# One trunk layer of an mLSTM, Conformer and DiT hybrid: seven products for eight in two more f tiles, the convolution norm's rows spread by transfers, and four smaller edits

## The chip, the cores and the metric

The kernel runs on one core of one Trainium2 chip. The metric is the device time of one execution in microseconds; lower is better. The engines are named as the profile names them: PE is TensorE (matrix products), DVE is VectorE, ACT is ScalarE, POOL is GpSimd, and SP is SyncE, which here only issues transfers.

## What is computed

One layer runs over 128 context tokens and 512 latent tokens with the same weights, in float32. `D_MODEL` is 1024, `D_FF` 2816, the mLSTM has 4 heads of 128, the Conformer branch 512 channels and a convolution of 31 taps.

```python
h = rmsnorm(x, p['norm1_g']) * (1 + sc1) + sh1
proj = jnp.einsum('btd,dc->btc', h, p['w_in']) + p['b_in']
q, k, v, o, i_f, f_f, i_b, f_b, u, ga, gb = jnp.split(proj, offs, axis=-1)
hA, st_f, st_b = mlstm_bidir(heads(q) * (DH_A ** -0.5), heads(k), heads(v),
                             gts(i_f), gts(f_f), gts(i_b), gts(f_b), st_f, st_b)
...
branch_a = jnp.einsum('bte,ed->btd', jax.nn.sigmoid(o) * hA, p['w_proj_a'])
ua, ub = jnp.split(u, 2, axis=-1)
z = dwconv1d(ua * jax.nn.sigmoid(ub), p['conv_dw_w'], p['conv_dw_b'])
z = jax.nn.silu(layernorm(z, p['conv_ln_g'], p['conv_ln_b']))
branch_b = jnp.einsum('bte,ed->btd', z, p['w_proj_b'])
merged = jax.nn.sigmoid(ga) * branch_a + jax.nn.sigmoid(gb) * branch_b
x = x + g1 * jnp.einsum('btd,de->bte', merged, p['w_out'])
h2 = rmsnorm(x, p['norm2_g']) * (1 + sc2) + sh2
gate, val = jnp.split(jnp.einsum('btd,df->btf', h2, p['w_up']), 2, axis=-1)
gate = dwconv(gate)          # 3x3 on the latent grid, width 3 on the context
x = x + g2 * jnp.einsum('btf,fd->btd', jax.nn.gelu(gate) * val, p['w_down'])
y = rmsnorm(x, final_norm_g)
```

The six modulation vectors (`sc1`, `sh1`, `g1` and their like) come from a linear map of SiLU(c). Outputs are y and the mLSTM's final context state.

## The kernel before

**Layout.** x stands feature-major: eight tiles of 128 features by 640 tokens. All weights are one array of blocks of 128 x 128, in the order in which they are used; eight blocks are a group (`GB`, 512 KB). SP loads groups into a ring of three tiles, `wst` (`load`, L459).

**Products.** Every large product is made from two roundings of each operand, a high part and the low rest. `prep` (L474) makes them of a weight group: ACT copies `wst` to `wh`; the low part `wl` is either `wst - wh` on DVE, or, for the groups in the set `TWICE` (L163), ACT writes the negative of the copy to `wl` and POOL issues a transfer that adds the group from device memory (`in_w`) to it. `three_of` (L623) then issues three matmuls for each block and each half of 320 tokens: high by high, high weight by low input, low weight by high input. The `h` of the input projection is split alike into `hh` and `hl`, those of the FFN stand in one tile `h`, or `hx` below.

**Order.** Each engine works its instructions in program order. The order is made while the program is built: `_Order` (L187) keeps a clock of its own for each engine, with a cost for each operation (`cost`, L220). Between the matmuls it resumes generators (`od.spawn`), which yield until what they wait for is ready by that clock (`until`, L305) or until DVE is not too far ahead (`room`, L313), and it fills DVE with small pieces of background work (`later` and `fill`, L339 and L342): the taps of both convolutions and the products of the later modulation, `junk` in the profile.

**Stages.** Input projection in the order of `ORDER` (u, g, k, q, ...; k and q with number 2 are the third heads'), the mLSTM beside it, then both branches (`BRANCH`), w_out, the FFN, and the final norm.

**The convolution norm** (`conv_norm`, L1260) is a layer norm over 512 channels, which lie in the partitions of four tiles z. PE sums over partitions (`colsum_into`, L665: a row of 656 columns as 4 groups of 164, at partitions 0, 32, 64 and 96), DVE makes the mean `mu`, and `bcast` (L670) spreads that row over all partitions by four matmuls into two PSUM tiles, from which DVE subtracts, in halves of 328 columns. The squares are summed in the same way, and `bcast` spreads the reciprocal deviation.

**The FFN.** D_FF is 22 f tiles of 128. A tile's up projection gives gate and value, 128 x 640 each. For f below `NPL` (L57) `ffn_tile` (L1628) makes it with eight products per pair of k blocks and two token halves, 96 matmuls in all. For the others `ffn_pair` (L1638) makes it with seven, in the way of Strassen: gate and value rows, and the two halves of tokens, form a 2 x 2 scheme over each pair of k blocks. The seven weight forms are A11, S1, S2, A12, S3, S4, A22 (`FORMS`); S1 to S4 are sums and differences of weights, `sf` in the profile, made and split by `prep_form` (L505): for S1 and S3 the low part is made on DVE, for the others by an adding transfer of POOL's. They meet the input forms B11, T1, T2, B21, T3, B22, T4. B's are quarters of h2. T1 to T4 are differences of them, 4 forms for 4 k pairs, that is 16 tiles `hx`. The generator `up_forms` (L1501) makes them: DVE the difference (`hf`), ACT its high part, DVE the low part (`hx<-hf,hx`). They come in the order T1, T3, T2, T4 for the first k pair, then for the next. `ffn_pair` waits for all of them in the order's clock (`od.finish(t_uf)`) before it issues its products. Each product of a weight form runs over its four k pairs, 4 x 3 = 12 matmuls. The gate is collected in `gbuf`, the nine taps of its convolution are DVE's (`acc`). Parts of the down product stand between f tiles (`DN_AT`): the first one behind f4.

**The end.** The down product's last part runs over the tokens in two parts, 384 and 256. `final` (L1749) norms each part: sums over partitions by `colsum_into`, `rstd` (L681) with a reciprocal and four small operations on DVE, a spread by matmuls, and the products that give y.

**PSUM** is set up by `psum_pools` (L392): a pool `mm` for products and a pool `ps` for all else.

## Time and profile before

| what | us |
|---|---|
| runs | 949.36, 950.96, 951.27 |
| median | 950.96 |
| the profiled execution | 950.29 |
| its span | 948.5 |
| PE busy in it | 914.2 |
| DVE busy | 742.1 |
| ACT busy | 531.6 |
| POOL busy | 130.6 |

The span runs from the first to the last recorded instruction; times in the profile count from its start. All instructions go through one helper, so the profile gives the line L182 for nearly all of them, and they are told apart by tile names: `mm<-hx,wl` is a product into PSUM tile mm of the inputs hx and wl. A row of the timeline gives start, duration, engine, line, operation and tiles; a run of like instructions is one row with its count. In square brackets stands how long the engine sat idle before it and what ended that.

### The profile page before, as it was taken

To read this page: it belongs to the slowest core of one execution; us is meant where nothing else is said; L and a number is where in the kernel's file an instruction comes from. 1 tells how busy PE (TensorE), PEld (TensorE's weight loads), DVE (VectorE), ACT (ScalarE), POOL (GpSimd) and SP (SyncE) were. 2 spreads that over 40 slices of the span, in tenths; PEclk is the share of its full clock that TensorE was granted. 3 is DMA by queue.
4 is the path that set the end of the run, shared out by engine and by line. 5 is a ranking of instruction groups with operands and counts; after the bars stand their busy time and mean duration, and the time that the engine had idled before them with its cause. 6 is when DMAs were issued, how large, how long until landed. Compare 5 with 4: busy or idle time off the path is not lost.

```text
span 948.5 us, 16981 instructions
## 1 busy us (share of the span) xinstructions
PE 914.2 (96%) x6456; PEld 893.0 (94%) x6456; DVE 742.1 (78%) x1540; ACT 531.6 (56%) x995; POOL 130.6 (14%) x181
## 2 busy tenths in 40 slices
PE   5999997999999999999999999999999999999995
PEld 2899997999999999999999999999999999999995
DVE  3829777887857988889788996877778877878666
ACT  5564575267758222223478766646765666666662
POOL 0001212000000000000000112222222222222210
PEclk9999999899999999999999999999999999999998
DMA  9638939543215646667544769887888889889975
GB/s 356 264 121 170 241 96 264 129 101 89 79 46 166 202 154 196 205 204 257 172 156 133 166 143 201 169 179 169 183 171 183 174 172 183 176 175 185 206 166 150
DMA packets 65954, 164.90 MB, mean 174 GB/s; under 512 B 6864, under 2 KB 15824, under 8 KB 65872
## 3 DMA queue, kind: packets, MB, share of 16 engines
q1 hardware_dynamic: 41360, 113.20, 37.0%
q0 software_dynamic: 24512, 50.60, 31.5%
q8 instruction: 51, 0.84, 0.4%
q14 instruction: 31, 0.25, 0.1%
HBM read 151.39 MB, written 3.48 MB: 163 GB/s over the span
## 4 chain that ended last, share of the span: by engine, by line
PE 83%; DMA 6%; DVE 4%; ACT 3%; issue 2%; SPq 0%; DVEq 0%; POOLq 0%; POOL 0%; ACTq 0%
PE mm L182 64%; PE ps L182 19%; DMA wl<-in_w 2%; DMA E<-in_mask 1%; DMA rowM<-M 1%; DMA out_ocst<-cs 1%; DMA x<-in_xT 1%; ACT L182 1%; DMA E<-rowM 1%; DVE x L182 0%; ACT z L182 0%; SPq L182 0%; DVE wl L182 0%; DMA cb<-in_crow 0%; DVE bc L182 0%
## 5 line engine op out<-in xcount | busy, mean ns | idle before, releaser
L182 ACT ACTIVATE wh<-wst 128x1024 fp32r<-128x1024 f32 (+1 forms) x114 | 114.1, 1007 | 99.2 <-PE mm L182 85.9
L182 DVE SCALAR_TENSOR_TENSOR acc<-gbuf,cols,acc 128x455 f32<-128x455 f32 (+2 forms) x176 | 129.7, 740 | 14.8 <-ACT acc L182 12.4
L182 PE MATMUL mm<-hh,wl 128*128 128x320 f32 (+2 forms) x576 | 134.8, 313 | 5.6 <-DMA wl<-in_w 5.6
L182 PE MATMUL mm<-hh,wh 128*128 128x320 f32 (+2 forms) x576 | 134.3, 312 | 2.9 <-ACT hh L182 1.6
L182 PE MATMUL mm<-hl,wh 128*128 128x320 f32 (+2 forms) x576 | 134.9, 313 | 0.0
L182 DVE SCALAR_TENSOR_TENSOR z<-glu,cols,z 128x641 f32<-128x641 f32 (+14 forms) x120 | 102.4, 887 | 22.6 <-ACT z L182 21.6
L182 POOL DMA_DIRECT2D wl<-in_w x69 | 60.9, 883 | 390.3 <-ACT wl L182 225.5
L182 PEld LDWEIGHTS mm<-hh,wl 128*128 128x128 f32 x576 | 97.0, 190 | 7.1 <-DMA wl<-in_w 5.9
L182 PEld LDWEIGHTS mm<-hh,wh 128*128 128x128 f32 x576 | 97.7, 190 | 4.8 <-ACT hh L182 2.1
L182 PEld LDWEIGHTS mm<-hl,wh 128*128 128x128 f32 x576 | 97.1, 190 | 1.8 <-issue 1.3
L182 PE MATMUL mm<-h,wh 128*128 128x320 f32 x452 | 85.5, 310 | 1.4 <-ACT h L182 0.8
L182 DVE SCALAR_TENSOR_TENSOR junk<-ad,cb 128x512 bf16<-128x512 f32 x128 | 82.0, 685 | 0.0
L182 DVE TENSOR_TENSOR wl<-wst,wh 128x1024 fp32r<-128x1024 f32 x55 | 67.1, 1221 | 17.2 <-ACT wh L182 17.1
L182 PE MATMUL mm<-al,wh 128*128 128x320 f32 (+2 forms) x336 | 80.5, 309 | 0.0
L182 PE MATMUL mm<-ah,wh 128*128 128x320 f32 (+2 forms) x336 | 80.3, 309 | 0.0
L182 PE MATMUL mm<-ah,wl 128*128 128x320 f32 (+2 forms) x336 | 80.3, 308 | 0.0
L182 ACT ACTIVATE wl<-wst 128x1024 fp32r<-128x1024 f32 (+1 forms) x91 | 74.3, 840 | 4.7 <-PE mm L182 4.7
L182 PEld LDWEIGHTS mm<-h,wh 128*128 128x128 f32 x452 | 71.2, 188 | 2.7 <-DVE h L182 1.2
L182 PE MATMUL mm<-h,wl 128*128 128x320 f32 x364 | 73.1, 309 | 0.3 <-DMA wl<-in_w 0.3
L182 DVE SCALAR_TENSOR_TENSOR x<-mm,mods,x 128x128 f32<-128x128 f32 (+1 forms) x168 | 63.7, 433 | 8.1 <-PE mm L182 7.5
L182 PEld LDWEIGHTS mm<-h,wl 128*128 128x128 f32 x364 | 58.5, 188 | 0.6 <-DMA wl<-in_w 0.6
L182 PEld LDWEIGHTS mm<-ah,wh 128*128 128x128 f32 x336 | 57.2, 188 | 0.1
(249 smaller groups left out, 1930.6 us busy)
## 6 DMA issues: line engine op xcount, KB each, us to landing
wst<-in_w SPq DMA_DIRECT2D x138, 512.0 KB, 4.5
wl<-in_w POOLq DMA_DIRECT2D x47, 512.0 KB, 7.2
ad<-in_ada SPq DMA_DIRECT2D x64, 256.0 KB, 3.1
adst<-in_ada SPq DMA_DIRECT2D x16, 512.0 KB, 10.2
wf<-in_w POOLq DMA_DIRECT2D x23, 256.0 KB, 5.0
wh<-sf POOLq DMA_DIRECT2D x22, 256.0 KB, 5.3
wl<-in_w POOLq DMA_DIRECT2D x22, 256.0 KB, 6.0
x<-in_xT SPq DMA_DIRECT2D x16, 320.0 KB, 5.8
```

What stands on the lines that cost most here:

```text
L182: return fn(*args, **kw)
```

## The change

1. `NPL` goes from 5 to 3: the f tiles 3 and 4 (the fourth and fifth) are made by `ffn_pair`. The wait for the sixteen T forms therefore comes at f3 and not at f5.
2. The weight groups of k and q with number 2 leave `TWICE`: DVE makes their low part from the tile in SBUF, where ACT's second copy and POOL's transfer made it.
3. Where each PSUM tile is one bank, the pool `ps` is opened before `mm`, so their banks change places.
4. Of the squares of x, tiles 3, 4, 5 and 7 are made by DVE; the first group's split stands behind the first `mrows`.
5. `on_all` takes the place of `bcast` in the convolution norm: SP writes the row to device memory (`zrow`) and reads it back into all partitions (`zb`). DVE subtracts and multiplies 656 columns at once, from SBUF.
6. The end's second part sums with tokens in the partitions (`token_sums`, two columns in place of 64), and `token_rows` spreads the result by two matmuls with the identity.

```diff
-NPL = 5
+NPL = 3
...
+TWICE -= {_g for _g in _IN if BLOCKS[_g * GB][0] in ("k", "q") and BLOCKS[_g * GB][2] == 2}
...
-        pools["mm"] = st.enter_context(tc.tile_pool(name=f"mm{nmm}", bufs=nmm, space=bass.MemoryType.PSUM))
-        pools["ps"] = st.enter_context(tc.tile_pool(name=f"ps{nps}", bufs=nps, space=bass.MemoryType.PSUM))
+        for nm, n in (("mm", nmm), ("ps", nps))[::-1 if banks == 1 else 1]:
+            pools[nm] = st.enter_context(tc.tile_pool(name=f"{nm}{n}", bufs=n, space=bass.MemoryType.PSUM))
...
+    def token_sums(pc, tile_, w, first, last):
+
+        n = w // P
+        for c in range(n):
+            PE.matmul(pc[:, c:c + 1], lhsT=tile_[:, c * P:(c + 1) * P], rhs=ones32[:, 0:1], start=first and c == 0,
+                      stop=last and c == n - 1)
+
+    def token_rows(r, a, b):
+
+        pt = ps()
+        for c in range(a, b):
+            PE.matmul(pt[:, (c - a) * P:(c - a + 1) * P], lhsT=r[:, c:c + 1].to_broadcast([P, P]), rhs=ident,
+                      start=True, stop=True)
+        return pt[:, 0:(b - a) * P]
...
-        S.activation(sq, x[j], AF.Square)
-        if j == 3:
+        if j in (3, 4, 5, 7):
+            V.tensor_mul(sq, x[j], x[j])
+        else:
+            S.activation(sq, x[j], AF.Square)
+        if j == 2:
...
-    prep(0)
...
+    prep(0, wait=False)
+    od.force(lines[0])
...
+    def on_all(r):
+
+        d = dz.tile([4, nz], F32, tag="row", name="zrow")
+        Q.dma_start(d, r[0:P:32, :])
+        t = A([P, TF], name="zb")
+        Q.dma_start(t, d.rearrange("g n -> (g n)").unsqueeze(0).to_broadcast([P, TF]))
+        return t
...
-        mb = bcast(mu, nz)
+        mb = on_all(mu)
...
-            for h in range(2):
-                s = slice(2 * nz * h, 2 * nz * (h + 1))
-                V.tensor_sub(z[m][:, s], z[m][:, s], mb[h])
+            yield from od.until(mb)
+            V.tensor_sub(z[m], z[m], mb)
...
-        rb = bcast(rz, nz)
+        rb = on_all(rz)
+        yield from od.until(rb)
...
-        n = (s.stop - s.start) // 4
-        pc = yield from sums_in(sums, adds, n)
+        if h == 0:
+            n = (s.stop - s.start) // 4
+            pc = yield from sums_in(sums, adds, n)
+        else:
+            n = (s.stop - s.start) // P
...
+            token_sums(pc, sums[0], n * P, True, False)
...
+            token_sums(pc, sums[1], n * P, False, True)
+            pc = pc[:, 0:n]
...
-        rb = bcast_part(r3)
+        rb = bcast_part(r3) if h == 0 else token_rows(r3, 0, n)
```

How the order of instructions changes at three places follows. The lines of the new kernel stand one further down (L183).

PE at the start of f3, before. `h2` are the quarters of the normed input, `wh` and `wl` a weight group's parts; gate and value are made one after the other, each from all eight k blocks and both token halves:

```order
L182 MATMUL mm_6063<-h2_5294,wl_5894 128x320
L182 MATMUL mm_6064<-h2_5643,wl_5894 128x320
L182 MATMUL mm_6134<-h2_5280,wh_5963 128x320
L182 MATMUL mm_6135<-h2_5636,wh_5963 128x320
L182 MATMUL mm_6134<-h2_5280,wl_5964 128x320
L182 MATMUL mm_6135<-h2_5636,wl_5964 128x320
L182 MATMUL mm_6134<-h2_5282,wh_5963 128x320
```

PE at the same place in the new kernel, behind f2's last two matmuls: A11, S1 and S2 (each row is three matmuls of one k pair):

```order
L183 MATMUL ps_6170<-h2_5246,wh_5933 128x320 x3
L183 MATMUL ps_6170<-h2_5250,wh_5933 128x320 x3
L183 MATMUL ps_6170<-h2_5254,wh_5933 128x320 x3
L183 MATMUL ps_6170<-h2_5258,wh_5933 128x320 x3
L183 MATMUL mm_6171<-hx_5772,wl_5937 128x320 x3
L183 MATMUL mm_6171<-hx_5949,wl_5937 128x320 x3
L183 MATMUL mm_6171<-hx_6074,wl_5937 128x320 x3
L183 MATMUL mm_6171<-hx_6136,wl_5937 128x320 x3
L183 MATMUL ps_6170<-hx_5851,wh_6038 128x320 x3
L183 MATMUL ps_6170<-hx_6001,wh_6038 128x320 x3
L183 MATMUL ps_6170<-hx_6115,wh_6038 128x320 x3
L183 MATMUL ps_6170<-hx_6154,wh_6038 128x320 x3
```

Behind f2 PE now meets twelve matmuls of A11 and then the T forms of all four k pairs, where 48 + 48 matmuls of h2 stood.

DVE from the twelfth T form, before; `hx<-hf,hx` is one T form's low part, `acc` the taps of a gate's convolution, `junk` the modulation's products:

```order
L182 TENSOR_TENSOR hx<-hf,hx 128x320
L182 TENSOR_TENSOR hf<-hf 128x320
L182 TENSOR_TENSOR al<-ge,ah 128x640
L182 SCALAR_TENSOR_TENSOR acc<-gbuf_5605,cols,acc 128x648 x2
L182 SCALAR_TENSOR_TENSOR acc<-gbuf_5605,cols,acc 128x455
L182 TENSOR_TENSOR hx<-hf,hx 128x320
L182 TENSOR_TENSOR hf<-hf 128x320
L182 SCALAR_TENSOR_TENSOR acc<-gbuf_5605,cols,acc 128x455 x2
L182 TENSOR_TENSOR hx<-hf,hx 128x320
```

DVE from the fifteenth T form in the new kernel:

```order
L183 TENSOR_TENSOR hx<-hf,hx 128x320
L183 SCALAR_TENSOR_TENSOR junk,modp<-ad,cb 128x512
L183 TENSOR_TENSOR hf<-hf 128x320
L183 SCALAR_TENSOR_TENSOR junk,modp<-ad,cb 128x512
L183 TENSOR_TENSOR hx<-hf,hx 128x320
L183 SCALAR_TENSOR_TENSOR junk,modp<-ad,cb 128x512
L183 TENSOR_TENSOR sf<-wst 128x512
L183 TENSOR_TENSOR sf<-wst,sf 128x512
L183 SCALAR_TENSOR_TENSOR junk,modp<-ad,cb 128x512 x2
L183 TENSOR_TENSOR mods<-modp 128x16
L183 TENSOR_TENSOR mods<-mods,cols 128x16
L183 TENSOR_TENSOR wh<-sf,wh 128x512
```

The taps between the last forms are gone, since f3's gate comes later; pieces of `junk` stand between them, and behind them the sums of the weight forms S3 and S4 and the low part of S3 (`wh<-sf,wh`).

DVE in the input projection, before: the end of a GLU (`glu`) and the convolution's taps (`z`):

```order
L182 SCALAR_TENSOR_TENSOR glu_1740<-gt_1738,gy_1590 128x512
L182 SCALAR_TENSOR_TENSOR z_1241<-glu_1196,cols_81,z_1241 128x652
L182 SCALAR_TENSOR_TENSOR z_1241<-glu_1196,cols_81,z_1241 128x653
L182 SCALAR_TENSOR_TENSOR z_1786<-glu_1740,cols_81,z_1786 128x641
L182 SCALAR_TENSOR_TENSOR z_1241<-glu_1196,cols_81,z_1241 128x654
L182 SCALAR_TENSOR_TENSOR z_1786<-glu_1740,cols_81,z_1786 128x642
```

DVE there in the new kernel:

```order
L183 SCALAR_TENSOR_TENSOR glu_1742<-gt_1740,gy_1592 128x512
L183 TENSOR_TENSOR wl_1747<-wst_1387,wh_1746 128x1024
L183 SCALAR_TENSOR_TENSOR z_1243<-glu_1198,cols_81,z_1243 128x652
L183 SCALAR_TENSOR_TENSOR z_1243<-glu_1198,cols_81,z_1243 128x653
L183 SCALAR_TENSOR_TENSOR z_1795<-glu_1742,cols_81,z_1795 128x641
L183 SCALAR_TENSOR_TENSOR z_1243<-glu_1198,cols_81,z_1243 128x654
L183 SCALAR_TENSOR_TENSOR z_1795<-glu_1742,cols_81,z_1795 128x642
L183 TENSOR_TENSOR wl_1813<-wst_1600,wh_1812 128x1024
```

The low parts of k's group (`wl_1747`) and q's (`wl_1813`) with number 2 stand among the taps; POOL's queue loses their two transfers.

More of the change, by code (lines that the diff above doesn't have):

```diff
@@ L432, in tile_trunk @@
     HALF = [slice(0, TH), slice(TH, T)]
+    PARTS = [slice(0, TL), slice(TL, T)]
     cols = cp.tile([P, NCOLS], F32, name="cols")
@@ L472, in wtile, with prep @@
         return od.ring(tag, (wf[0] if tag == "wf" else wp).tile([P, GB * P], F32R, tag=tag, name=tag), CAPS[tag])
-    def prep(g, tags=("wh", "wl")):
+    def prep(g, tags=("wh", "wl"), wait=True):
         if g in ready or g >= NGRP:
@@ L484, in parts @@
         def parts():
-            yield from od.until(src)
+            if wait:
+                yield from od.until(src)
             S.activation(hi, src, AF.Copy)
@@ L1258, in tile_trunk @@
     zs = {}
+    dz = ctx.enter_context(tc.tile_pool(name="dz", bufs=2, space=bass.MemoryType.DRAM))
+    def on_all(r):
[4 more added lines that the diff above has]
+        return t
     def conv_norm():
@@ L1294, in conv_out @@
     def conv_out(m, rb):
-        for h in range(2):
-            s = slice(2 * nz * h, 2 * nz * (h + 1))
-            V.tensor_mul(z[m][:, s], z[m][:, s], rb[h])
+        V.tensor_mul(z[m], z[m], rb)
         yield
@@ L1745, in tile_trunk @@
     ks = LASTF
-    PARTS = [slice(0, TL), slice(TL, T)]
     def final(h, sums, adds):
         s = PARTS[h]
-        n = (s.stop - s.start) // 4
-        pc = yield from sums_in(sums, adds, n)
+        if h == 0:
[3 more added lines that the diff above has]
+            n = (s.stop - s.start) // P
+            while not all(t[2] for t in adds[:-1]):
+                yield
+            yield from od.until(sums[0])
+            pc = ps()
+            token_sums(pc, sums[0], n * P, True, False)
+            while not adds[-1][2]:
+                yield
+            yield from od.until(sums[1])
+            token_sums(pc, sums[1], n * P, False, True)
+            pc = pc[:, 0:n]
         r3 = rstd(pc, n, 1.0 / D, "rs")
@@ L1763, in final @@
         for j in range(0, KD, 2):
-            t = A([P, 2, 4 * n], name="yo")
+            t = A([P, 2, n * P], name="yo")
             for i in range(2):
```

## Prediction

> **What bounds the kernel now.** I read the page first, then the busy time by windows, PE's waits, and last the timelines of the places where PE stands still. The page says that TensorE is the bound nearly throughout:
>
> ```profile
> span 948.5 us, 16981 instructions
> PE 914.2 (96%) x6456; PEld 893.0 (94%) x6456; DVE 742.1 (78%) x1540; ACT 531.6 (56%) x995; POOL 130.6 (14%) x181
> PEclk9999999899999999999999999999999999999998
> ```
>
> PE is busy for 914.2 of 948.5 us, so about 34 us is all that PE waits. The windows (span, busy time of each engine, PE's granted clock) show where: 10.4 us in the first 20.5 us, 9.8 us after the last product, nothing at all from 576 to 845.
>
> ```profile
> 0.00:20.50 20.50, 10.11 (x108) 4.02 (x108) 6.19 (x25) 12.36 (x20) 0.71 (x16) 1.00 0.91 348
> 540.00:575.20 35.20, 35.20 (x242) 35.20 (x241) 32.59 (x66) 22.80 (x42) 6.91 (x8) 1.00 0.77 170
> 576.00:845.00 269.00, 269.00 (x1834) 268.80 (x1833) 206.84 (x396) 167.06 (x319) 71.42 (x83) 1.00 0.83 174
> 936.00:948.50 12.50, 2.69 (x25) 2.13 (x24) 6.84 (x18) 1.09 (x3) 0.00 (x0) 0.63 0.43 149
> ```
>
> What lies outside the span is 950.29 - 948.5 = 1.8 us; the profiled execution, 950.29, is 0.67 below the median of the runs, 950.96. My sum is made against 950.29. What a measurement of this kernel can tell from no change is 0.2%, 1.9 us, so it takes a gain or a loss of that much to be seen.
>
> PE's waits between start and end have one large entry, and one that the order of the PSUM pools bears on:
>
> ```profile
> PE mm L182 <- DMA wl<-in_w: 6.0, 2, 5.6
> PE mm L182 <- DVE ga L182: 1.4, 2, 1.0
> ```
>
> **Seven products for eight, the gain.** In the window 540 to 575.2 PE is never idle and runs 242 matmuls, all but two of a plain f tile's or down product's kind: 35.2 / 242 = 0.1455 us each; 576 to 845 gives 269.0 / 1834 = 0.1467. A plain tile issues 96 such matmuls, a pair tile 7 x 4 x 3 = 84. Two tiles save 24: 24 x 0.147 = **3.5 us**, if PE stays fed.
>
> **Seven products, the price.** A pair tile needs the sixteen T forms of h2 that `up_forms` makes (`hx`), and each needs two VectorE subtractions (`hf`, then `hx`). Before, the first pair tile is f5. On PE it starts here (twelve matmuls of A11, then S1 on `hx`):
>
> ```profile
> 575.07 1.92 PE L182 MATMUL ps<-h,wh 128*128 128x320 f32 x12
> 576.82 1.47 PE L182 MATMUL mm<-hx,wl 128*128 128x320 f32 x9
> ```
>
> Counting back 48 matmuls of the down part and 2 x 96 of f4 and f3, 240 x 0.1463 = 35.1 us, f3 starts at 540.0. VectorE's timeline shows the forms 13 to 16 of 16 far behind that (only some rows):
>
> ```profile
> 548.98 2.56 DVE L182 SCALAR_TENSOR_TENSOR acc<-gbuf,cols,acc 128x648 f32<-128x648 f32 x3 [0.39 <-ACT acc L182]
> 551.46 0.48 DVE L182 TENSOR_TENSOR hx<-hf,hx 128x320 fp32r<-128x320 f32 x1
> 551.86 0.48 DVE L182 TENSOR_TENSOR hf<-hf 128x320 f32<-128x320 f32 x1
> 552.26 1.42 DVE L182 SCALAR_TENSOR_TENSOR acc<-gbuf,cols,acc 128x455 f32<-128x455 f32 x2
> ...
> 558.67 0.49 DVE L182 TENSOR_TENSOR hx<-hf,hx 128x320 fp32r<-128x320 f32 x1
> 559.07 0.69 DVE L182 SCALAR_TENSOR_TENSOR junk<-ad,cb 128x512 bf16<-128x512 f32 x1
> 559.68 0.08 DVE L182 DVE_READ_ACCUMULATOR junk<-ad,cb 128x1 f32 x1
> 559.80 0.17 DVE L182 TENSOR_TENSOR mods<-modp 128x16 f32<-128x16 f32 x1
> ```
>
> Form 13 (T1 of the last k pair) begins at 551.46 and form 16 at 558.67. Before, that leaves 16 us until f5; now f3 wants them, 35 us earlier than f5. What VectorE does up to form 13 hardly changes. By the order of its rows between forms 1 and 13, three taps of f3's convolution go (two of 648, one of 455 elements: the 548.98 group, 2.5 us) and three weight forms of 128x512 come (`sf`, `sf`, `wl`), by the first row here, of the tile's view, 3 x 0.68 = 2.05 us (the last row is the page's, for transfers of half the size of a group, median us to landing at its end):
>
> ```profile
> L182 DVE TENSOR_TENSOR sf<-wst x34: 681/684/689, 560.8 to 873.6; 128x512 f32<-128x512 f32 x34
> L182 ACT ACTIVATE wh<-sf x50: 612/622/632, 570.5 to 875.4; 128x512 fp32r<-128x512 f32 x50
> wh<-sf POOLq DMA_DIRECT2D x22, 256.0 KB, 5.3
> ```
>
> So form 13 starts at about 551.2 and ends at 551.7, in the clock of the trace of before. From there VectorE alternates: a form's step of `hx` 0.40, `hf` 0.40 and two `junk` of 0.61 is 2.0 us, so form 15 ends at 555.7 and 16 at 557.8. One `junk` later (558.3) come the sums of S3 and S4, ending 559.0 and 559.6; two more `junk`, two `mods` and then S3's low half end at 562. PE meanwhile: A11 and three quarters of S1 from 540.0 to 543.1, then waits for form 13 until 551.7 (**8.6**); the rest of S1 and three quarters of S2 to 553.5, waits for form 15 until 555.8 (**2.3**); S2's rest and A12 to 558.0, waits for S3's low half until 562 (**4.0**); S3 to 563.8. S4's low half is a copy on ACT (0.62) and an adding transfer of GpSimd's, issued about 561 and landing 5.3 us later or somewhat more, 566.8: waits **3.0**. Then S4 and A22. Sum 17.9 us, and f4's forms arrive about when wanted. Where PE stands this long its clock falls (next part); most of the half-speed time lies inside the later waits, since VectorE and not PE dates them, and I add 1: **19 us**, bounds 14 (GpSimd's and S3's waits half as long) and 21.
>
> **The rows of k2 and q2.** The 5.6 us wait, on PE, on GpSimd (POOL) and on VectorE:
>
> ```profile
> 160.26 0.46 PE L182 MATMUL mm<-hl,wh 128*128 128x320 f32 x2
> 166.35 0.90 PE L182 MATMUL mm<-hh,wl 128*128 128x320 f32 x2 [5.63 <-DMA wl<-in_w]
> 152.56 1.55 POOL L182 DMA_DIRECT2D E<-in_mask  x1 [2.49 <-DMA E<-rowM]
> 153.53 1.59 POOL L182 DMA_DIRECT2D wl<-in_w  x1
> 163.15 0.86 POOL L182 DMA_DIRECT2D wl<-in_w  x1 [4.03 <-ACT wl L182]
> 148.12 0.89 DVE L182 SCALAR_TENSOR_TENSOR glu<-gt,gy 128x128 f32<-128x128 f32 x2
> 155.27 9.75 DVE L182 SCALAR_TENSOR_TENSOR z<-glu,cols,z 128x641 f32<-128x641 f32 x12 [4.52 <-ACT z L182]
> L182 DVE TENSOR_TENSOR wl<-wst,wh 128x1024 fp32r<-128x1024 f32 x55 | 67.1, 1221 | 17.2 <-ACT wh L182 17.1
> 164.50:171.20 6.70, 4.85 (x18) 4.85 (x19) 6.70 (x10) 0.00 (x0) 0.00 (x0) 0.50 0.97 233
> wl<-in_w POOLq DMA_DIRECT2D x47, 512.0 KB, 7.2
> ```
>
> k2's low half is queued on POOL behind the mask transfers and lands when PE has waited 5.6 us. Now VectorE makes it, right behind the glu pair at 148.1 to 149.8: done at 151.1, in VectorE's own idle stretch before 155.27. q2's stands three taps further, done at 159, wanted at 164. Gain 5.6. The clock is 0.50 for 164.5 to 171.2 and the 18 matmuls in it take 4.85 us where 18 x 0.147 = 2.6 would do: 2.2 more. Next late would be k3's transfer, issued 163.15, landing by the median 7.2 us at 170.4, wanted at about 174 once PE is no longer held up: **7.8 us**, bounds 4 (k3's late, clock not quite full) and 7.8.
>
> On the page "TensorE: Matmul & The Clock Gate", Part 1, the Trainium skill states that TensorE drops to half clock after an idle window of about 3.4 us, and comes back after about 3.4 us of sustained work. The drop agrees with the row of 164.5; the return took longer here, since PE worked from 166.3 to 171.2 at half clock, 4.9 us. That rule speaks against the pair tiles: each long wait in f3 would be followed by up to 3.4 us at half speed, 1.7 us lost; by it, with the first wait's loss in full, the result would be 0.7 later than my sum.
>
> **Convolution norm.** PE loses two spreads; the first is the second row:
>
> ```profile
> 264.57 1.32 PE L182 MATMUL ps<-z,ones 128*32 128x164 f32 x32
> 267.28 1.28 PE L182 MATMUL ps<-mu,sel 128*128 128x164 f32 x8
> 271.71 0.49 PE L182 MATMUL ps<-zsq,ones 128*32 128x164 f32 x8
> DMA to landing us min/median/max: 3.4/3.8/4.9
> ```
>
> The row holds 1.0 us of own time (the rest is pipeline): **2.0 us** off PE for both. The price: mean, row write, row read, subtraction and square must be over before PE reaches the squares' sums. The nearest transfer is the spread of `in_crow` over all partitions, 3.4 to 4.9 us to landing (the last line, of tile `cb`); two in a row are 7 to 10. In the new order some 64 matmuls stand between the z sums and the first square's sum where 7.1 us lay before, about 10 us; less mean, subtraction and square, 8 us are left. Value 0, bounds 0 to 3 for the first spread. The second has slack until the projections. On SP both row transfers stand ahead of a weight load, which is held until the row is written; a ring of three groups, each 7 us of PE's work (48 x 0.147), covers the 4 to 5 us. The four operations of 656 columns on z replace eight of 328: nothing.
>
> **Pools and end.** With PSUM tiles placed the other way, the first projection product may no longer wait for `ga`'s bank: **1.0**, bounds 0 and 1.4. The end's chain shrinks from 64 columns to 2:
>
> ```profile
> 938.45 0.22 DVE L182 TENSOR_SCALAR rsv<-ps 128x64 f32<-128x64 f32 x1 [0.71 <-ACT rsy L182]
> 938.59 0.54 DVE L182 RECIPROCAL rsy<-rsy 128x64 f32<-128x64 f32 x1
> 940.06 1.94 PE L182 MATMUL ps<-rsy,sel 128*128 128x64 f32 x8 [2.02 <-DVE rsy L182]
> ```
>
> Eight spreading matmuls (1.94) become two with 128 columns each (by the same row 2 x 0.48 for twice the columns at most), which saves 1.0. An operation of 16 columns took 0.17 us above (559.80), so I estimate the reciprocal on two columns at 0.2 for 0.54 and four small operations at 0.17 for 0.22: **1.4** with a little taken off for the transposing sums, bounds 0.8 and 2.0. At the start the squares of x are shared between ACT, busy 12.36 of the first 20.50 us, and VectorE, busy 6.19, and the first group's split moves behind the first `mrows`: ACT has it off its hands earlier, but PE there waits for x to arrive in any case: **0.2**, bounds -0.5 and 0.5.
>
> **How the numbers follow.** Gains 3.5 + 7.8 + 2.0 + 1.0 + 1.4 + 0.2 = 15.9. Price 19. Net 3 us slower: 950.3 + 3.1 = **953.4 us**.
>
> **Rivals.**
> - *The T forms are in time* (ends faster). VectorE would have to finish form 13 by 543, eight us sooner: if the wait for PE and ACT at the start of the forms shrank, or the order let the forms overtake the taps. For it speaks only that VectorE idles 35.20 - 32.59 = 2.6 us in the window of 540; against it the order of its rows, which leaves no place for eight. Then the price is nil: 950.3 - 15.9 = 934.4. It decides when form 13 ends before 543. Chance 0.12.
> - *Half the price.* VectorE is right but S3's and S4's weights are ready sooner and the clock stays up, or PE, having less to do before, leaves VectorE more slack: price 8 to 12, 942 to 946. Chance 0.16.
> - *A new wait in the front half.* k3's transfer comes late or the spreads hold PE for 3 us and more, so that some 4 to 6 of the 15.9 are not got: 957 to 960. Chance 0.17.
> - *The forecast*: 0.55, its own range 949 to 957.
>
> The range: 940 to 960 leaves out the first rival and little at the other end. Faster by over 0.2% (under 949.1): the first two rivals nearly whole, 0.26, and 0.06 of the forecast's low side: 0.32. Slower (over 952.9): 0.33 of the forecast and 0.14 of the third rival: 0.47. The rest, 0.21, lies within.
>
> **What would show it.** In the profile after: PE idle 8 us at the second product of f3, released by VectorE's `hx`, then 2 to 4 us three times, clock 0.5 there; no wait for `wl<-in_w` near 160; no `ps<-mu,sel`; some 3.5 us less of PE work up to f5. If PE's idle time in f3 is below 10 us the price is wrong, and the time with it; if PE waits for `zsq` or for another `wl<-in_w`, the third rival is right.

## The result, and the profile after

The changed kernel takes 960.94 us (median of 4 runs, 959.51 to 964.23), the kernel before 950.25. The ratio is 1.0117, with a 95% interval of 1.0088 to 1.0146: slower by 10.7 us. The forecast was slower by 3.1, and the measured time lies 0.9 us above the end of its range. The stall in f3 was there, but it was longer, and in part PE waited for other things than forecast.

The page of the changed kernel, its span and the engines' busy time:

```profile
span 959.4 us, 16942 instructions
PE 914.3 (95%) x6404; PEld 890.0 (93%) x6404; DVE 758.2 (79%) x1558; ACT 535.0 (56%) x1009; POOL 134.0 (14%) x185
```

PE has 52 matmuls fewer on record and is as busy as before (914.2). So the 11 us of span are waits, and busy time in which a matmul took longer. PE's waits between 25 and 600 us, by what ended them (total, times, longest):

```profile
PE mm L183 <- ACT hx L183: 7.0, 1, 7.0
PE ps L183 <- ACT gbuf L183: 5.2, 1, 5.2
PE mm L183 <- DMA wf<-sf: 3.1, 1, 3.1
PE mm L183 <- DMA wl<-sf: 2.5, 1, 2.5
PE mm L183 <- DMA wl<-in_w: 1.9, 2, 1.6
PE mm L183 <- DVE va L183: 1.3, 1, 1.3
PE mm L183 <- DVE ga L183: 1.0, 1, 1.0
```

The 5.6 us for `wl<-in_w` at 166 are gone. In their place stand four waits, all in f3 and f4. The 1.6 us for `wl<-in_w` are those of another group, at 78.8; they come and go with the execution: e2 below, whose first half is that of the kernel before, has 1.6 there, and of e10 and e11, whose first halves are alike, only e10 has such a wait. The 1.0 for `ga` is still there. PE's timeline in f3 and at the end of f4 (the number behind x counts matmuls):

```profile
531.03 1.93 PE L183 MATMUL ps<-h,wh 128*128 128x320 f32 x12
532.79 1.50 PE L183 MATMUL mm<-hx,wl 128*128 128x320 f32 x9
541.32 1.43 PE L183 MATMUL mm<-hx,wl 128*128 128x320 f32 x3 [7.03 <-ACT hx L183]
547.96 1.17 PE L183 MATMUL ps<-hx,wh 128*128 128x320 f32 x3 [5.20 <-ACT gbuf L183]
...
558.77 1.78 PE L183 MATMUL mm<-h,wl 128*128 128x320 f32 x10 [2.49 <-DMA wl<-sf]
560.35 3.40 PE L183 MATMUL ps<-hx,wh 128*128 128x320 f32 x12
563.55 2.00 PE L183 MATMUL ps<-h,wl 128*128 128x320 f32 x12
...
576.02 1.92 PE L183 MATMUL mm<-h,wf 128*128 128x320 f32 x10 [3.13 <-DMA wf<-sf]
577.74 3.31 PE L183 MATMUL ps<-hx,wf 128*128 128x320 f32 x12
580.88 0.31 PE L183 MATMUL mm<-ah,wh 128*128 128x320 f32 x1
```

A11 runs at 531.03, three quarters of S1 follow, and PE stands still for the thirteenth T form, as forecast. S2 then does not wait for the fifteenth form, but for ACT's copy of A11 to `gbuf`. ACT's timeline there:

```profile
547.05 0.47 ACT L183 ACTIVATE hx<-hf 128x320 fp32r<-128x320 f32 x1 [1.63 <-DVE hf L183]
547.43 0.48 ACT L183 ACTIVATE gbuf<-ps 128x128 f32<-128x128 f32 x2
```

S2 adds into the PSUM tile that holds A11, so that tile must be copied first, and the copy stands behind the sixteenth form's high part in ACT's order. A11 was done at 533; its copy came at 547.4.

The windows show the granted clock inside the first wait, behind the second, and behind the third:

```profile
536.50:541.20 4.70, 0.00 (x0) 0.00 (x0) 4.64 (x11) 2.31 (x5) 0.00 (x0) 0.50 0.16 56
548.30:553.50 5.20, 5.20 (x21) 5.20 (x21) 3.76 (x11) 3.32 (x8) 1.72 (x2) 0.50 0.64 136
553.50:558.00 4.50, 2.78 (x19) 2.52 (x18) 2.51 (x5) 3.54 (x8) 1.08 (x2) 1.00 1.01 229
560.30:563.60 3.30, 3.30 (x15) 3.30 (x14) 2.61 (x5) 2.48 (x4) 0.00 (x0) 0.50 0.65 113
```

The clock falls to 0.50 while PE waits for the thirteenth form, is 0.50 while S2 and part of A12 run, and again while A22 of f3 runs: its twelve matmuls take from 560.35 to 563.55, 3.2 us for 1.76. A22 of f4, 577.74 to 580.88, has the same pace.

Four marks divide the run: PE's first product, the first z product (`mm<-zh`), the FFN's first product (`mm<-h`), f5's S1. Before they stood at 20.6, 336.1, 493.1 and 576.8 us, in the changed kernel at 22.8, 326.9, 484.0 and 589.6. So PE comes to the FFN 9.1 us earlier, needs 105.6 us for 83.7 from there to f5's S1, 21.9 more, and from there to the span's end 369.8 for 371.7, 1.9 less: -9.1 + 21.9 - 1.9 = 10.9, the difference of the spans.

### The profile page after: what moved, and what is told of

Its sections match the earlier page's. It is cut to its first block, busy times and chain, and to the rows that moved or that the text cites. A ratio compares the mean times of both kernels' runs of the same rounds, so it can differ in the third digit from the quotient of the medians.

```text
span 959.4 us, 16942 instructions
## 1 busy us (share of the span) xinstructions
PE 914.3 (95%) x6404; PEld 890.0 (93%) x6404; DVE 758.2 (79%) x1558; ACT 535.0 (56%) x1009; POOL 134.0 (14%) x185
## 4 chain that ended last, share of the span: by engine, by line
PE 84%; DVE 6%; DMA 4%; ACT 3%; issue 2%; SPq 0%; POOL 0%; DVEq 0%; POOLq 0%; ACTq 0%
PE mm L183 64%; PE ps L183 20%; DVE acc L183 2%; DMA wst<-in_w 1%; DMA wf<-sf 1%; DMA wl<-in_w 1%; DMA x<-in_xT 1%; ACT wh L183 1%; DVE hf L183 1%; DVE junk L183 1%; DVE wl L183 0%; DVE x L183 0%; DVE hx L183 0%; DMA wl<-sf 0%; ACT hf L183 0%
## 5 line engine op out<-in xcount | busy, mean ns | idle before, releaser
L183 ACT ACTIVATE wh<-wst 128x1024 fp32r<-128x1024 f32 (+1 forms) x122 | 116.6, 967 | 100.1 <-PE mm L183 92.8
L183 DVE SCALAR_TENSOR_TENSOR acc<-gbuf,cols,acc 128x455 f32<-128x455 f32 (+2 forms) x176 | 129.7, 740 | 13.7 <-ACT acc L183 11.2
L183 PE MATMUL mm<-hh,wh 128*128 128x320 f32 (+2 forms) x576 | 134.2, 312 | 2.5 <-ACT hh L183 1.6
L183 PE MATMUL mm<-hh,wl 128*128 128x320 f32 (+2 forms) x576 | 133.3, 310 | 1.9 <-DMA wl<-in_w 1.9
L183 PE MATMUL mm<-hl,wh 128*128 128x320 f32 (+2 forms) x576 | 133.5, 311 | 0.0
L183 DVE SCALAR_TENSOR_TENSOR z<-glu,cols,z 128x641 f32<-128x641 f32 (+14 forms) x120 | 102.6, 888 | 13.3 <-ACT z L183 12.2
L183 PEld LDWEIGHTS mm<-hh,wh 128*128 128x128 f32 x576 | 96.2, 188 | 5.4 <-ACT hh L183 2.5
L183 PEld LDWEIGHTS mm<-hh,wl 128*128 128x128 f32 x576 | 96.4, 188 | 3.6 <-DMA wl<-in_w 2.4
L183 PEld LDWEIGHTS mm<-hl,wh 128*128 128x128 f32 x576 | 96.5, 188 | 0.9 <-issue 0.4
L183 POOL DMA_DIRECT2D wl<-in_w x49 | 43.1, 879 | 352.1 <-ACT wl L183 178.0
L183 DVE TENSOR_TENSOR wl<-wst,wh 128x1024 fp32r<-128x1024 f32 x57 | 69.6, 1221 | 17.8 <-ACT wh L183 17.6
L183 DVE SCALAR_TENSOR_TENSOR junk<-ad,cb 128x512 bf16<-128x512 f32 x128 | 82.4, 686 | 0.1
L183 PE MATMUL mm<-ah,wh 128*128 128x320 f32 (+2 forms) x336 | 80.5, 310 | 0.5 <-ACT ah L183 0.5
L183 PE MATMUL mm<-h,wh 128*128 128x320 f32 x408 | 75.1, 311 | 1.9 <-ACT h L183 0.8
L183 PE MATMUL mm<-al,wh 128*128 128x320 f32 (+2 forms) x320 | 75.6, 309 | 0.4 <-DVE al L183 0.4
L183 DVE SCALAR_TENSOR_TENSOR x<-mm,mods,x 128x128 f32<-128x128 f32 (+1 forms) x168 | 63.7, 433 | 8.6 <-PE mm L183 7.5
L183 PEld LDWEIGHTS mm<-h,wh 128*128 128x128 f32 x408 | 63.6, 188 | 3.6 <-DVE h L183 1.2
L183 PEld LDWEIGHTS mm<-ah,wh 128*128 128x128 f32 x336 | 57.2, 188 | 0.9 <-ACT ah L183 0.8
L183 PE MATMUL ps<-hx,wf 128*128 128x320 f32 x348 | 57.0, 314 | 0.0
L183 PEld LDWEIGHTS mm<-al,wh 128*128 128x128 f32 x320 | 54.2, 188 | 0.7 <-DVE al L183 0.7
L183 PE MATMUL mm<-ah,wl 128*128 128x320 f32 (+2 forms) x224 | 54.7, 308 | 0.0
L183 ACT ACTIVATE wl<-wst 128x1024 fp32r<-128x1024 f32 (+1 forms) x66 | 53.9, 841 | 1.3 <-DMA wst<-in_w 1.3
```

What stands on the lines that cost most here:

```text
L183: return fn(*args, **kw)
```

## The experiments

Each kernel was timed beside the kernel before, several kernels in a batch. The kernel before alone had medians from 950.3 to 951.8 in the batches, so kernels of one batch are compared directly, and those of different batches with a microsecond or so of doubt. The marks are those of one profiled execution each. "FFN head" is the last mark less the one ahead of it.

| kernel | batch | median us | first product | z | FFN | f5's S1 | FFN head |
|---|---|---|---|---|---|---|---|
| before | 0 | 950.25 | 20.6 | 336.1 | 493.1 | 576.8 | 83.7 |
| changed | 0 | 960.94 | 22.8 | 326.9 | 484.0 | 589.6 | 105.6 |
| e1: rest, NPL 5 | 1 | 945.48 | 22.1 | 326.3 | 483.5 | 571.5 | 88.0 |
| e2: pairs only | 1 | 970.39 | 20.6 | 336.4 | 493.4 | 598.5 | 105.1 |
| e3: NPL 4 | 1 | 950.47 | 22.3 | 326.0 | 483.2 | 578.8 | 95.6 |
| e4: kept warm | 1 | 962.57 | 22.8 | 326.5 | 483.6 | 589.8 | 106.2 |
| e5: NPL 3, junk first | 2 | 963.94 | 23.1 | 334.2 | 501.9 | 596.7 | 94.9 |
| e6: NPL 5, junk first | 2 | 955.46 | 22.3 | 333.6 | 502.0 | 585.0 | 83.0 |
| e7: NPL 4, junk first | 2 | 961.80 | 22.7 | 330.0 | 497.5 | 589.3 | 91.8 |
| e8: e6, start undone | 2 | 952.67 | 20.9 | 328.3 | 495.6 | 579.0 | 83.4 |
| e9: NPL 5, junk later | 3 | 939.06 | 20.7 | 324.4 | 482.4 | 566.7 | 84.3 |
| e10: NPL 3, junk later | 3 | 949.03 | 20.2 | 323.2 | 481.1 | 577.0 | 95.9 |
| e11: e10, eased | 3 | 948.37 | 20.3 | 323.5 | 481.4 | 577.0 | 95.6 |
| e12: e9, k2 and q2 undone | 3 | 948.70 | 22.1 | 336.4 | 494.4 | 579.1 | 84.7 |
| e13: e9, norm undone | 4 | 939.78 | 20.8 | 328.0 | 485.8 | 568.3 | 82.5 |
| e14: e9, pools undone | 4 | 938.02 | 20.5 | 324.6 | 482.6 | 566.0 | 83.4 |
| e16: e9, start new | 4 | 940.15 | 22.4 | 326.1 | 484.1 | 568.5 | 84.4 |
| e17: e10, forms first | 4 | 947.71 | 22.1 | 325.2 | 483.1 | 577.3 | 94.2 |
| e18: e9 again | 5 | 938.76 | 22.4 | 326.1 | 484.1 | 567.5 | 83.4 |
| e19: e14 again | 5 | 939.23 | 20.5 | 326.9 | 484.8 | 569.5 | 84.7 |

### Which part costs: the rest alone, the pairs alone, one pair

e1 is the changed kernel with one number back:

```diff
-NPL = 3
+NPL = 5
```

> The changed kernel with NPL back at 5: f3 and f4 by eight products, all other edits kept. Theory (the two pair tiles cost 25.3 us from f3's S1 to f5's S1 and save 3.5; the rest of the change gains about 11): 950.3 - 11 = 939, down to 937 where the clock at the start comes up as early as in the profile of before. Rival (the pair tiles cost little, the rest of the change loses): at or above 950.

Measured 945.48, ratio 0.9934 (0.9916 to 0.9953): 5 us faster than before, where 11 were expected. The rival falls, but 6 us of the expected gain are missing. The marks say where: the FFN head takes 88.0 us for 83.7. PE's waits there, 500 to 600 us:

```profile
PE mm L183 <- DVE x L183: 2.7, 1, 2.7
PE ps L183 <- DMA wf<-sf: 0.9, 1, 0.9
```

DVE's timeline ahead of that `x` holds the last six junk products in one row. The first and the last of them, and what waits behind:

```profile
559.75 0.69 DVE L183 SCALAR_TENSOR_TENSOR junk<-ad,cb 128x512 bf16<-128x512 f32 x1
...
562.81 0.69 DVE L183 SCALAR_TENSOR_TENSOR junk<-ad,cb 128x512 bf16<-128x512 f32 x1
...
563.85 0.68 DVE L183 TENSOR_TENSOR sf<-sf,wst 128x512 f32<-128x512 f32 x1
...
565.65 1.13 DVE L183 SCALAR_TENSOR_TENSOR x<-mm,mods,x 128x128 f32<-128x128 f32 x3
```

The first down part needs the modulation `g2`, whose junk products were not done. Of the 128, 116 stand ahead of the first T form here and in the changed kernel, and 123 in the kernel before: PE, served earlier, left DVE less idle time to fill (from PE's first product to the first T form DVE was idle for 95.9 us before and for 86.4 here).

e2 is the kernel before with `NPL = 3` and no other edit.

> The kernel before with NPL 3 and nothing else. Theory: 950.3 + 25.3 - 3.5 = 972, all of it between f3 and f5. My forecast's own terms, 19 - 3.5, would give 966. Rival (the stall in f3 is only that PE comes to f3 earlier by the rest's gain, and DVE would have been in time): under 958, since here PE comes 9 us later to f3; but DVE's anchor moves with PE too.

Measured 970.39, ratio 1.0197 (1.0176 to 1.0218): the theory's 972, not my 966. The FFN head is 105.1 us, as in the changed kernel. The pair tiles' price does not come from PE being early.

e3 is the changed kernel with `NPL = 4`.

> The changed kernel with NPL 4: only f4 is a pair tile more. f3's eight products give DVE 14.1 us, so the forms are there. Theory: 1.76 us less of products than with NPL 5, and at S2, S3 and S4 of f4 waits of 1 to 4 in sum: 938 to 942, within 2 of the kernel with NPL 5. Rival (a pair tile that early costs by its weight forms, whichever tile it is): 10 us above the kernel with NPL 5, about 949.

Measured 950.47, 5 us above e1 (ratios to the kernel before 0.9996 and 0.9934). Neither number holds, the rival's is nearer. PE's waits in the FFN's head:

```profile
PE mm L183 <- DMA wl<-sf: 4.9, 1, 4.9
PE ps L183 <- ACT gbuf L183: 4.2, 1, 4.2
```

The thirteenth form is in time for f4, but the copy behind the sixteenth and S4's transfer are not.

### Is it the clock

e4 is the changed kernel with matmuls that fill the two first waits of f3; nothing else moves in any engine's order:

```diff
                 x = HX[i, xn]
+                if f == 3 and (n, i) in ((1, 3), (2, 0)):
+                    pw = mm_bank()[:, 0:TH] if n == 1 else pw
+                    for _ in range((44, 30)[n - 1]):
+                        nc.tensor.matmul(pw, lhsT=hi[:, 0:P], rhs=HX[0, "T1"][:, 0, :], start=True, stop=True)
```

> The changed kernel with 44 matmuls without use in front of S1's fourth product in f3 and 30 in front of S2's first, into a PSUM bank that nobody reads, so that PE does not stand still there; the outputs are untouched. Theory (the half clock behind the waits costs 2.3 us after S2 begins, and part of 1.4 later): 2 to 4 us faster than the changed kernel, 957 to 959. Rival (VectorE and ACT date these products, the clock costs nothing of its own): within 1 us of it, 961.

Measured 962.57 for 960.94, ratios 1.0119 and 1.0117: no gain, as the rival had it. The half clock behind the second wait is gone, but the next wait takes it over:

```profile
PE mm L183 <- DMA wl<-sf: 3.8, 1, 3.8
PE mm L183 <- DMA wf<-sf: 3.5, 1, 3.5
PE ps L183 <- ACT gbuf L183: 1.1, 1, 1.1
```

S4's transfer is waited for 3.8 us where it was 2.5, and now S4's matmuls behind that wait run at half speed:

```profile
557.58 3.03 PE L183 MATMUL mm<-h,wl 128*128 128x320 f32 x10 [3.76 <-DMA wl<-sf]
```

These ten took 1.78 us in the changed kernel. So S4 starts 1.2 us earlier and loses that again, and f4's S1 starts at 565.2 here and at 565.4 in the changed kernel. Filling the two waits wins nothing: S4 then waits longer for its transfer, and the half clock does not go away, it moves there. What f3 would take without any half clock, the run does not show. The half clock behind a tile's last wait, A22 of f3 and of f4, is 1.4 us each. Only f4's has no wait of f3 or f4 behind it; f3's stands ahead of f4's wait for its transfer, and no run shows how much of it is hidden there.

### DVE's leftover work

e5, e6 and e7 are the kernels with NPL 3, 5 and 4 and one number of the planner: how far ahead of PE DVE may be with junk. It is raised where these products begin:

```diff
         ada_cond()
+        od.slack = 900.0
         for n in range(NAD):
```

> The changed kernel (NPL 3) with one number of the planner raised where the later modulation's products begin (od.slack 900 for 450), so that all 128 junk products stand ahead of the first T form; in the changed kernel 12 stand behind it. Theory (DVE's leftover work dates the T forms, S3's and S4's sums): form 13 comes 2, form 16 about 5 us earlier; the two first waits, 7.0 and 5.2, shrink by about 6 in sum: 954 to 957. Rival (GpSimd's adding transfers and the clock date f3 and f4): within 2 of the changed kernel, 959 to 962.

> The kernel with NPL 5 and the rest of the change, junk first as well. In that kernel's run PE waited 2.7 us in the first down part and 0.9 in f5, and ran 1 us at half clock behind them, since twelve junk products stood in one row before the down part. Theory (that row is what gave back part of the rest's gain): 945.5 - 4.5 = 941. Rival (PE meets DVE at its limit there in any case): 944 to 946.

> NPL 4, the rest of the change, junk first. In the run with NPL 4 PE waited 4.2 us for ACT's copy behind form 16 in f4, then 4.9 for S4's transfer, and lost 3.8 at half clock. Theory: form 16 comes 5 us earlier, the first wait goes and with it most of what follows: 940 to 943. Rival (S4's transfer dates f4): 947 to 950.

Measured 963.94, 955.46 and 961.80: each slower than its counterpart, by 3.0 (for which the intervals of the ratios overlap), 10.0 and 11.3, and as medians all three expectations failed. (The row of junk in e1 that the second text counts as twelve holds six; twelve stand behind the first T form.) The marks show two effects apart. The FFN head shrinks as the theory said, and more: with NPL 5 from 88.0 to 83.0, with NPL 3 from 105.6 to 94.9, with NPL 4 from 95.6 to 91.8. But the first z product comes 4 to 7 us later, counted from the first product, the stretch from there to the FFN's first grows by 10 us and more, and PE's waits of e6 between 25 and 500 us name the place:

```profile
PE mm L183 <- ACT zh L183: 10.7, 2, 6.2
```

One of the two stands ahead of the first z product, the other behind it. With more junk ahead of it, the second half of the convolution norm comes late for the z products. The number was raised too early in the program.

e9 and e10 raise it only behind the convolution norm, with NPL 5 and 3, and have the start as before:

```diff
                 psum_pools(6, 2, 1)
+                od.slack = 2000.0
```

> NPL 5, the start as before, and the planner's lead for junk raised only behind the convolution norm (to 2000), so that all 128 junk products stand ahead of the first T form. The two kernels with the lead raised earlier lost 9 to 10 us at the first z products, where ACT's zh came late, and won 5 us between the FFN's first product and f5. Theory: the loss is gone and the 5 stay, the start gives 1.9: 945.5 - 4.6 - 1.9 = 939. Rival (DVE led by junk makes another stage late): 945 or above.

> The same with NPL 3. From the FFN's first product to f5's S1 the pairs' run with junk first took 94.9 us, that with NPL 5 and junk first 83.1: 11.8 more. Theory: the sum holds, 11.8 above the kernel with NPL 5 and junk later, 951 if that is 939. Rival (the pair tiles' price is all DVE's leftover junk): equal to it or faster.

Measured 939.06, ratio 0.9861 (0.9841 to 0.9880), against the theory's 939; and 949.03, ratio 0.9976 (0.9962 to 0.9990), 10.0 above it where 11.8 was expected. With NPL 3 PE's waits in the FFN's head are down to two of the four:

```profile
PE mm L183 <- ACT hx L183: 6.4, 1, 6.4
PE ps L183 <- ACT gbuf L183: 5.2, 1, 5.2
```

The waits for `wl<-sf` and `wf<-sf` went with the raised lead; the two first ones did not. In the changed kernel the sums of S3 and S4 stood behind leftover junk on DVE, but the lead moves more than junk: in e10 the sums of further weight forms also come ahead of the adds to `gbuf`, for which DVE waits for PE. e2 tells against the junk alone. Behind its first T form DVE's order is that of the changed kernel but for the modulation's work, 5 junk products where there are 12; yet its FFN head is 105.1 us, and PE waits there 3.7 us for `wf<-sf` and 7.3 for `gbuf`. How much of the 9.7 us by which e10's head is shorter is junk, and how much the order of the weight sums, no run separates.

### What stays: order or amount

e11 is e10 with the two waits eased that do not come from the forms: A11 is issued, and copied, ahead of the wait for the forms, and S4's low part is DVE's in f3 and f4:

```diff
-        od.finish(t_uf)
...
             read(n)
+            if n == 0:
+                od.finish(t_uf)
...
-            if nm[0] == "A" or nm in LO_DMA:
+            if nm[0] == "A" or nm in LO_DMA and not (nm == "S4" and PAIRS[g] < 5):
```

> As the kernel with NPL 3 and junk later, with two more edits: A11's product and ACT's copy of it to gbuf are issued ahead of the wait for the T forms, so that the copy no longer stands behind form 16's on ACT; and S4's low part of f3 and f4 is made by DVE, not by GpSimd's adding transfer. Theory (these two waits, not form 13's, are half of the price): 4 to 6 us faster than that kernel. Rival (form 13 to 16 date everything): within 1 us of it.

Measured 948.37 against 949.03: the rival's. The copy now comes early, the wait for it falls from 5.2 to 1.5 us, and the wait for the thirteenth form grows from 6.4 to 10.7, as DVE has `sf` and `wf` work of f3 ahead of the forms.

e17 is e10 with the taps of the FFN's convolution held back until the forms are issued:

```diff
     t_uf = od.spawn(up_forms())
+    od.tap_slack = -1500.0
...
         od.finish(t_uf)
+        od.tap_slack = SLACK
```

> The kernel with NPL 3, start as before and junk later, with the convolution's taps held back by the planner (tap_slack -1500) until the T forms are issued: between forms 1 and 13 stand 17 taps and 2 ge for 24 and 6. Theory (what is left of the price is the place of the forms behind taps): form 13 comes 7 us earlier, f3's two waits of 6.4 and 5.2 and 2.4 us at half clock shrink by 6 to 10: 939 to 943. Rival (DVE has no room: the taps held back make gbuf or the down part late instead): 947 or above.

Measured 947.71, ratio 0.9969 (0.9956 to 0.9982) for e10's 0.9976: at the edge of the rival's, no clear gain over e10, and not the theory's 939 to 943. The thirteenth form starts at 534.4 instead of 537.5, 51.2 us behind the FFN's first product instead of 56.4, and no product waits for a form any more. PE's waits have another name:

```profile
PE ps L183 <- ACT gbuf L183: 6.9, 3, 4.7
PE mm L183 <- ACT gbuf L183: 2.1, 1, 2.1
```

Only the 2.1 are for the taps: ACT's copy into `gbuf` at 525.4 waits 1.6 us until DVE's `acc` has read what stands there. The 4.7 are S2's of f3, again for the copy of A11, which was done at 535.0. PE's row, and ACT's rows ahead of that copy:

```profile
541.44 3.27 PE L183 MATMUL ps<-hx,wh 128*128 128x320 f32 x12 [4.66 <-ACT gbuf L183]
...
538.56 0.47 ACT L183 ACTIVATE hx<-hf 128x320 fp32r<-128x320 f32 x1 [1.22 <-DVE hf L183]
538.94 1.13 ACT L183 ACTIVATE wh<-wst 128x512 fp32r<-128x512 f32 x2
540.37 0.63 ACT L183 ACTIVATE wf<-sf 128x512 fp32r<-128x512 f32 x1 [0.30 <-DVE sf L183]
540.91 0.48 ACT L183 ACTIVATE gbuf<-ps 128x128 f32<-128x128 f32 x2
```

The copy stands behind the sixteenth form and three weight copies in ACT's order. e11 has the copy early and the forms late, e17 the forms early and the copy late. The two edits together were not run, so whether the rest of the price is the amount of DVE's work ahead of f3 or its order stays open.

### The other edits

e12 is e9 with the groups of k and q 2 back in `TWICE`.

> As the kernel with NPL 5, start as before and junk later, with k2's and q2's low parts back on ACT and GpSimd. Theory (my term for this edit): 7.8 us slower than that kernel. Rival (k3's transfer or another takes the wait's place, so that less was won): 3 to 5 slower.

Measured 948.70, 9.6 above e9 in the same batch. My 7.8 was got in full and 1.8 more: besides the wait of 5.4 us, smaller ones come back.

```profile
PE mm L182 <- DMA wl<-in_w: 7.5, 3, 5.4
PE mm L182 <- DVE va L182: 2.0, 1, 2.0
PE mm L182 <- DVE ga L182: 1.5, 2, 1.0
PE ps L182 <- ACT kw L182: 1.0, 1, 1.0
```

Against e9 these are 1.7 for `wl<-in_w`, 1.6 for `va`, 1.0 for `ga` and 0.4 for `kw`.

e13 is e9 with `bcast` in the convolution norm, in place of `on_all` (edit 5 undone). e14 opens the pools as before (edit 3 undone).

> The kernel with NPL 5, start as before and junk later, with the convolution norm's rows spread by matmuls again. My term for that edit: 2.0 us slower than the kernel it is taken from. Rival (the two row transfers hold PE or ACT somewhere, or PE had a wait there that now takes the place): within 0.7 of it.

> The same kernel with the PSUM pools opened in the order of before. My term: 1.0 us slower. Rival: equal, since the traces after still show the 1.0 us wait of the first z product for ga; then the edit was worth nothing.

Measured 939.78 and 938.02, in another batch than e9. Between the first product and the first z product e13 needs 307.2 us for e9's 303.7, 3.5 more, of which 1.4 is a wait for `wl<-in_w` that e9's execution did not have; the other 2.1 fit my term. e9's median is only 0.7 below e13's, but it is of another batch. Within the batch e13 is 1.8 above e14 (939.28 to 939.86 against 937.40 to 938.44); the two differ in edits 3 and 5, and edit 3 turns out below to make no difference that can be told (the medians of e18 and e19 are 0.5 apart), so edit 5 gave about 1.8 of my 2.0. The row's way through device memory is covered, as taken. SP's timeline of the changed kernel for the first spread, and the landing of the reads:

```profile
262.14 0.57 SPq L183 DMA_DIRECT2D zrow<-mu  x1
263.79 0.33 SPq L183 DMA_DIRECT2D zb<-zrow  x1
...
DMA to landing us min/median/max: 3.9/4.1/4.3
```

From the write's issue to the read's landing, 263.79 + 3.9, are 5.6 us where I had 7 to 10 against 8 of cover; no wait of PE for `zsq` is in the profile. For the pools, e18 and e19 repeat e9 and e14 side by side:

> The kernel with NPL 5, start as before and junk later once more, beside the next one on the same chip: 938 to 940.

> The same with the PSUM pools in the order of before, once more. Apart the two gave 939.1 and 938.0 in different calls. If the order of the pools is worth my 1.0, this is 1 slower; if it costs, 1 faster; if nothing, within 0.5.

Measured 938.76 and 939.23, intervals 0.9849 to 0.9887 and 0.9863 to 0.9901: no difference that these runs can tell. Edit 3 is worth nothing, and the wait for `ga` of 1.0 us stands in both profiles.

The start: e8 is e6, and e16 is e9, with one start for the other.

> As the kernel with NPL 5 and junk first, but with the start as before: all squares of x on ACT, the first group's split where it was. In the profiles so far PE's first product stands at 20.6 without the edit (two kernels) and at 22.1 to 22.8 with it (four kernels). Theory (the edit delays the start, since PE's clock comes up later): 1.5 to 2 us faster than the kernel it is taken from. Rival (a matter of the execution): within 0.5 of it. My forecast, 0.2 slower, is the rival's.

> The same kernel with the start of the changed kernel (four squares on DVE, the first split later). Theory: 1.5 to 2.8 us slower, first product at 22 or later in the profile. Rival (chance, as the run with k2 undone had its first product at 22.1 with the old start): within 0.7.

e8 is 2.8 us faster than e6 in the same batch, but in the profiled executions only 1.4 us of the difference lies ahead of the first product, and 3.9 between there and the first z product. e16 is 1.1 slower than e9, which ran in another batch, and 2.1 slower than e14, which ran in the same batch and differs besides only by edit 3. The new start had its first product at 22.1 to 23.1 in all eight profiles, the old one at 20.2 to 20.9 in nine and at 22.1 to 22.4 in three (e12, e17, e18). The medians of e9 and e18 agree within 0.3 though their profiled starts differ by 1.8. The edit costs, by these, between 1 and 3; how much is not settled.

## Why the forecast was right in direction and wrong in size

**The pair tiles' price**, 19 us, is the term that failed, if the run is divided by the marks. From f3's A11 to f5's S1 PE took 589.6 - 531.0 = 58.6 us; before it was 576.8 - 540.0 = 36.8, less 3.5 for the 24 matmuls saved 33.3. The price is 25.3. Term by term, forecast and measured:

| term | forecast | measured |
|---|---|---|
| S1 waits for form 13 | 8.6 | 7.0 |
| S2 waits | 2.3, for form 15 | 5.2, for ACT's copy of A11 |
| S3 waits for its low half | 4.0 | 0 |
| S4 of f3 waits for its transfer | 3.0 | 2.5 |
| f4 | 0 | 3.1, S4's transfer |
| half clock | 1 | 4.9 |
| sum | 18.9 | 22.7 |

The half clock is S2 and A12 (21 matmuls in 5.2 us, 2.1 over 21 x 0.147) and the two A22 (1.4 each). The rest of 2.6 lies in S1's last three matmuls, which took 1.43 us at half clock, and in small pieces that I can't place.

Three steps failed. "S2's rest ... waits for form 15": form 15 was indeed there in time, but I read only DVE's order, and what S2 adds to is released by ACT, in ACT's order: 5.2 us, and with the copy early (e11) 1.5. "f4's forms arrive about when wanted": the T forms did, but not f4's weight forms; I stopped the working by hand at the end of f3, though DVE and GpSimd were still behind. And "I add 1" for the clock: that it is hidden where a later wait dates the product was right in the main for S2 and A12 (with both at full speed in e4, S4's matmuls start only 1.2 us earlier), but I did not ask what follows the last wait of a tile; behind f4's nothing hides it. S3's wait of 4.0 did not come at all: S2 began late, and S3's low half was there by then.

**Counted from e1** the account looks otherwise. On top of e1 the pair tiles cost 960.94 - 945.48 = 15.5 us, and with the 3.5 saved 19.0, my price. That is luck: the terms under it are wrong one by one, as the table shows. On this count it is the rest that failed, 5.1 us where my terms add up to 12.4, and the larger part of that is a loss that I put at nothing: PE comes earlier to an FFN for which DVE is not ready, and e1's head is 4.3 us longer than before. With the pair tiles that loss lies within their waits: in e2 PE comes to the FFN no earlier than before, and the head is as long as in the changed kernel (105.1 for 105.6).

What I saw but did not weigh was that the junk stands among the forms because DVE had not come round to it earlier. I counted six junk products in the order and took them as given; e9 and e10 show that a greater lead for junk shortens the FFN head by about 4 us with NPL 5 (88.0 to 84.3) and about 10 with NPL 3 (105.6 to 95.9), the latter not by the junk alone, as e2 shows.

**The front part.** -11.0 was forecast up to the FFN's first product, -9.1 measured. The start is the difference: +2.2 in this execution and not -0.2. k2 and q2 gave more than forecast (9.6 for 7.8 by e12), the norm about 1.8 of its 2.0 (e13 against e14), the pools nothing for 1.0.

**The end.** From f5's S1 to the span's end 1.9 were won for 1.4. The last chain is as forecast: from the start of PE's last product to the end of the span it took 12.7 us before and 11.2 after.

**The rivals.** The third rival came nearest to the time (957 to 960, measured 960.9), but for a reason that it did not name, which is luck: k3's transfer was not late, PE did not wait for `zsq`, and what was missing was missing in the FFN and at the start. The first one, forms in time, would have needed DVE 7 us earlier; e17 brought the thirteenth form 5 us closer to the FFN's first product and found ACT's copy of A11 in the way. On the clock the Trainium skill ("TensorE: Matmul & The Clock Gate", Part 1) has half speed for about 3.4 us of work behind an idle window: the row of 560.3 (3.3 us at 0.50) agrees; behind the second wait it was longer, from S2's start at 547.96 to 553.5. The 1.7 us for each long wait that I had worked out from it as an estimate would have been nearer than my 1 for all of them.

The version that beats both kernels is e9: edits 2, 3, 5 and 6, NPL 5, the old start, and junk ahead of the FFN. It takes 938.8 to 939.1 us, with ratios of 0.9861 and 0.9868 to the kernel before. e14, without edit 3, is its equal.

## What to carry to other kernels

Where a product writes over a buffer that another engine must first read out, follow that reader's place in its own engine's order, not only the operands. Saving work on the engine that bounds a stage can cost more than it brings when another engine has that stage nearly filled: DVE was busy 92.6% of the window ahead of f5, and the two pair tiles, to save 3.5 us on PE, asked for the T forms 35 us earlier. When a gain in front shortens idle time that background work used, look for that work further on; here moving it took one number and shortened the FFN head with NPL 5 by 4 to 5 us, but it won time only where the number was raised behind the stage that needs DVE promptly. And when two edits each ease one half of a wait, run them together before the wait is called the price of the work.

## What was not expected of the hardware

PE at the start. The spread of x's first statistics is eight matmuls of 160 columns. In the kernel before:

```profile
16.19 1.35 PE L182 MATMUL ps<-rsy,sel 128*128 128x160 f32 x8 [1.28 <-DVE rsy L182]
20.57 0.56 PE L182 MATMUL mm<-hh,wh 128*128 128x256 f32 x2 [1.59 <-ACT hh L182]
```

In the changed kernel:

```profile
15.97 2.50 PE L183 MATMUL ps<-rsy,sel 128*128 128x160 f32 x8 [0.65 <-DVE rsy L183]
22.77 0.55 PE L183 MATMUL mm<-hh,wh 128*128 128x256 f32 x2 [1.60 <-ACT hh L183]
```

The statistics come 0.2 us earlier, as I had forecast, and then the same eight matmuls take 2.50 us for 1.35, so that the first product is 2.2 later. This divides all twenty profiles: the eight matmuls take 2.50 us in the eleven with the first product at 22.1 or later and 1.35 in the nine others. Three of the eleven (e12, e17, e18) have the old start, so one order of instructions can run at either pace. The durations are those of a slower clock, yet the column of the granted clock has 1.00 there in both profiles: at the start it does not tell these two apart, and the durations do.

The clock also fell behind a short wait. In the kernel before, PE waited 2.15 us for `va` up to 112.69, and this window follows:

```profile
113.30:116.60 3.30, 3.30 (x18) 3.30 (x17) 3.30 (x7) 2.97 (x11) 0.00 (x0) 0.50 1.07 189
```

So here a wait of 2.15 us, shorter than the idle window of about 3.4 us that the Trainium skill ("TensorE: Matmul & The Clock Gate", Part 1) names, was followed by 3.3 us at half speed; the waits of 2.49 and 3.13 us ahead of the changed kernel's two A22 were as well.
